# Moved fills, a tile and a buffer more, and gates one tile early in a hybrid recurrent layer on one core

## The chip, the cores and the metric

The kernel runs on one core of one Trainium2 chip. The metric is the device time of one execution in microseconds; the time given is the median of several runs. Engines are called by the names of the profile: PE (TensorE, matmul), DVE (VectorE), ACT (ScalarE), POOL (GpSimd) and SP (SyncE, which issues nearly all the DMAs).

## What is computed

One layer of a decoder, float32, for two groups of tokens: a prompt of 256 tokens and 8 samples of 8 tokens each, 320 token columns in all. Cut to what matters here:

```python
h = rms_norm(x, norm_g)                       # x: 320 x 2048
p = h @ w_in                                  # 2048 x 12416: all of both branches' inputs and gates
# branch A (RWKV-7, 16 heads of 64): token shift, low-rank decay and input gate, then per token
#   S = S diag(w) - (S kk)(kk * a)^T + v k^T ;  y = S r
# branch B (HGRN2, 8 heads of 128), per token
#   S = diag(g) S + k v^T ;  o = S^T q
y_a = (group_norm(y) * ln_w + ln_b + bonus) * silu(p[za])
y_b = rms_norm(o, hg_g) * silu(p[zb])
merged = sigmoid(p[GA]) * (y_a @ proj_a) + sigmoid(p[GB]) * (y_b @ proj_b)
y = rms_norm(x + merged @ w_out, final_norm_g)
```

The states of both branches after the last token are outputs too. The samples start from given states (`state_rwkv`, `state_hgrn`), the prompt from zero.

## The kernel before

Activations are kept transposed: 128 channels on the partitions, 320 tokens in the columns. Each float32 product of the large projections is made of three fast products: the weights `raw` are split by ACT into a rounded high part (`whi`) and by DVE into the rest (`wlo`), the activations likewise (`hhi`, `hlo`), and PE adds `whi*hhi`, `whi*hlo` and `wlo*hhi`. One tile of a projection is 128 output columns; its 16 blocks of 128 inputs are 48 matmuls of 128 x 320. Weights come in pieces of 8 blocks (512 KB) into three buffers. The work has four stages.

*Start.* The three pieces of `x` (piece 2 holds the 64 sample tokens) are squared and summed by ACT (`squares`, `scale`), scaled by DVE (`gain`, line 643), transposed by PE (`turn`, line 655), and split into `hhi` (ACT, `high`) and `hlo` (DVE, `low`). Meanwhile POOL builds masks (`mf`, `mk`, `own8`) and then the low parts of the first weights (`half`, line 750; `divide`, line 535). The order on PE, ACT, DVE and POOL is written out by hand here. `first` is the first tile of the projection; `fetch(0, 0, 1)` loads the next weights into a buffer as soon as POOL has finished with it. A run of fills (lines 700 to 709) writes constants into tiles that the recorded stage uses later: `yz`, `xc`, `qz`, halves of `lora_lw` and `lora_la`, and the masks `rs_a` and `rs_b` of the scans.

*Recorded stage* (lines shown as L199 in the profile, whichever function issues them). 71 tiles of the input projection stream through PE, and between them goes the work of eight pairs: two heads of branch A (`rwkv(p, ...)`) and one of branch B (`hgrn(p, ...)`) each. All instructions are first recorded with their reads and writes, and `Recorder.order` then plans one order for each engine and the SP queue from the dependences, a cost for each instruction and the rank of what hangs on it. For a POOL operation of this kind its cost line is

```python
o.cost = 950 if "dma" in name else 95 + free * 0.88 if name == "memset" else (330 if name == "tensor_copy" and free > 9 else 200) + free * 1.66
```

to which 20 is added and 65 taken off. Tiles of branch A come from `at(...)`: a tag with `bufs` buffers that go round; calls with the same tag share them. Small products go to PSUM banks whose tiles are all called `bank` in the profile.

In `rwkv`, `s0` is the state of the eight samples: loaded by SP, transposed by PE (`ps0`), scaled in place by DVE, added to, and stored by SP. The scaling factors reach the right places through PE: POOL writes them on diagonals (`fd`, 128 x 256, twice for each pair, from `fq`), and PE multiplies `jr_sum` with `fd` into `pf`. At the end of a pair the output `py` is split into `yh` and `yl` (high and low part), which PE multiplies with `jr_cent`; squares are split into the same two tiles, and PE multiplies them with `jr_mean`. `yl` takes the tag `fd`, which has one buffer.

*Projections and gates* (lines 1616 to 1641). The outputs `ya` and `yb` are split (`split`: `yah`, `yal`, `ybh`, `ybl`). Then follow 16 tiles of 128 output channels. For each: gate A (`ga`; the first seven were computed in the recorded stage, stored to `late`, and are loaded here), gate B (`gbt`, a tile of the input projection and a sigmoid of three ACT steps), the projection of A (`ppa`), that of B (`ppb`), and the merge on DVE and ACT (`mt`, `mhi`, `mlo`, `ms`).

*Output projection* (lines 1662 to 1781), with the residual and the last norm.

Of the kernel before, what the change touches and what calls it, by code (L numbers as in the profile page):

```python
# [9 lines left out]
F32 = mybir.dt.float32  # L10
F32R = mybir.dt.float32r
# [6 lines left out]
NP_ = 256  # L18
NS = 64
NT = NP_ + NS  # L20
NSEQ = 8
LS = 8
KT = D // 128
# [404 lines left out]
def hybrid_step(ctx, tc, x_prompt, x_sample, state_rwkv, state_hgrn, state_shift, norm_g, w_in,  # L428
# [4 lines left out]
    V, S, G, T = nc.vector, nc.scalar, nc.gpsimd, nc.tensor  # L433

    S.add_instruction(mybir.InstLoadActFuncSet(
        name=nc.get_next_instruction_name(), act_func_set_id=EXP_LN_SET, ins=[], outs=[]))
# [11 lines left out]
    def ctile(shape, name, dt=F32, pool=rconst):  # L448
        return pool.tile(shape, dt, name=name, tag=name)
# [12 lines left out]
    lora_lw = ctile([128, NT], "lora_lw", F32R)  # L462
    lora_la = ctile([128, NT], "lora_la", F32R)
# [3 lines left out]
    HS = [slice(0, 64), slice(64, 128)]  # L467
# [18 lines left out]
    def project(dst, w, c0, nk, xhi, xlo, pre=()):  # L486

        for k8 in range(nk // 8):
            hi, lo = pre[k8] if k8 < len(pre) else weights(load(w, c0, k8))
            for q in range(8):  # L490
                k = 8 * k8 + q
                T.matmul(dst, hi[:, q, :], xhi[:, k, :], start=(k == 0), stop=False)  # L492
                T.matmul(dst, hi[:, q, :], xlo[:, k, :], start=False, stop=False)  # L493
                T.matmul(dst, lo[:, q, :], xhi[:, k, :], start=False, stop=(k == nk - 1))  # L494
                yield

    def run(gen):
        for _ in gen:
            pass
# [3 lines left out]
    def main(c0, post, pre=()):  # L503
        ps = psm.tile([128, 512], F32, name="mps", tag="m")
        yield from project(ps[:, :NT], win, c0, KT, hhi, hlo, pre)
        post(ps[:, :NT])


    with tc.tile_pool(name="start", bufs=1) as st, \
# [21 lines left out]
        def divide(b_, n, sub):  # L531
            for j in range(n):
                ks = slice(8 * j // n, 8 * (j + 1) // n)
                S.copy(whi[b_][:, ks], wraw[b_][:, ks])
                sub.tensor_sub(wlo[b_][:, ks], wraw[b_][:, ks], whi[b_][:, ks].bitcast(F32))
            return whi[b_], wlo[b_]
# [132 lines left out]
        def warm(n):  # L669
            for _ in range(n):  # L670
                T.matmul(wps[:, :256], ones[:, :128], ones, start=True, stop=True)

        tps = {}
        with tc.manual_schedule(engines={mybir.EngineType.PE, mybir.EngineType.Activation, mybir.EngineType.DVE,
# [20 lines left out]
            yz = ctile([128, 2, 2, 2, 64], "yz")  # L695
            xc = ctile([128, 4, 32], "xc")
            qz = ctile([128, NSEQ, 32], "qz")
            arp = ctile([128, 5, 2, 2, 64], "arp")
            for t_ in (yz, xc, qz, lora_lw[HS[1]].bitcast(F32), lora_la[HS[0]].bitcast(F32)):
                V.memset(t_, 0.0)  # L700


            rs_a = ctile([128, NT], "rs_a")
            rs_b = ctile([128, NT], "rs_b")
            V.memset(rs_a, 1.0)
            V.memset(rs_a[:, 0:NP_:64], 0.0)
            V.memset(rs_a[:, NP_::8], 0.0)
            V.memset(rs_b, 1.0)
            V.memset(rs_b[:, ::8], 0.0)
            warm(20)  # L710
            squares(2)
            scale(2)
# [26 lines left out]
            def first(part, k4):  # L739

                w, x = ((whi, hhi), (whi, hlo), (wlo, hhi))[part]
                for k_ in range(4 * k4, 4 * k4 + 4):
                    T.matmul(first_ps[:, :NT], w[k4 // 2][:, k_ % 8], x[:, k_], start=part == 0 and k_ == 0,
                             stop=part == 2 and k_ == KT - 1)
# [39 lines left out]
            first(1, 2)  # L784
            first(2, 2)
            divide(2, 1, G)
            V.memset(arp, 0.0)
            ps = pst.tile([128, 512], F32, name="cps", tag="t")
            T.transpose(ps[:, :128], rows, ident)
# [29 lines left out]
    def sigm(out, in_, bias=0.0, sign=1.0):  # L819

        S.activation(out, in_, AF.Exp, scale=-sign, bias=bias)
        S.activation(out, out, AF.Ln, bias=1.0)
        S.activation(out, out, AF.Exp, scale=-1.0)
# [12 lines left out]
    def ring(pool, tag, shape, bufs, dt, size, clear=False):  # L836

        if (pool.name, tag) not in rings:
            n_ = size or math.prod(shape[1:])
            if tag in SHARED:  # L840
                rings[pool.name, tag] = [0, [wide_[:, SHARED[tag]:SHARED[tag] + n_]]]
                if clear:
                    G.memset(wide_[:, 384:], 0.0)
        if (pool.name, tag) not in rings:
            rings[pool.name, tag] = [0, [pool.tile([128, n_], dt, name=f"{tag}_{j}", tag=f"{tag}_{j}")
                                         for j in range(bufs)]]
            for t_ in rings[pool.name, tag][1]:
                if clear:
                    G.memset(t_ if dt == F32 else t_.bitcast(F32), 0.0)
        r_ = rings[pool.name, tag]  # L850
        t_ = r_[1][r_[0] % len(r_[1])]
        r_[0] += 1
        t_ = t_[:shape[0], :math.prod(shape[1:])]
        if len(shape) == 2:
            return t_
        names = "abcdef"[:len(shape) - 1]
        return t_.rearrange(f"p ({' '.join(names)}) -> p {' '.join(names)}", **dict(zip(names, shape[1:])))
# [7 lines left out]
    def at(name, shape=(128, NT), tag=None, bufs=1, dt=F32):  # L865
        tag = tag or name
        return ring(pa, tag, list(shape), bufs, dt, SIZES.get(tag), tag in CLEAR)
# [48 lines left out]
    def rwkv(p, r, k, v, za):  # L916
# [6 lines left out]
        for dst, own, other in ((wst, HS[0], HS[1]), (ast, HS[1], HS[0])):  # L923
            S.copy(dst[own], w2a2[own])
            V.tensor_sub(dst[other], w2a2[own], dst[own].bitcast(F32))
        s0 = at("s0", (128, NSEQ, 64))
        Y.dma_start(s0, state_rwkv[0, :, 2 * p:2 * p + 2].rearrange("s h v k -> (h v) s k"))

        kk = at("kk", (128, 3, 128), tag="uK").rearrange("p a b -> p (a b)")[:, :NT]
# [141 lines left out]
        for i in range(1, 7):  # L1071
            m = 7 - i
            t_ = at("t3", (128, 5, i, m), tag="big")
# [6 lines left out]
        t_ = at("t3", (128, 4, 8, 8), tag="big")  # L1080
        V.tensor_mul(t_, within(0, [264, 4], [32, 8], [1, 8]), own8[:, None, None, :].to_broadcast([128, 4, 8, 8]))
        V.tensor_reduce(column(0, [40, 4], [1, 8]), t_, axis=mybir.AxisListType.X, op=ALU.add)
        for d_ in range(1, 4):
            n, m = 4 - d_, 8 * d_
            pw_ = at("pw_", (128, n, 8), tag="uK")
            t_ = at("t3", (128, n, 8, m), tag="big")
            V.tensor_mul(t_, within(8, [264, n], [32, 8], [1, m]), column(32 * d_ + 8, [40, n], [0, 8], [1, m]))
            V.tensor_reduce(pw_, t_, axis=mybir.AxisListType.X, op=ALU.add)
            t_ = at("t3", (128, n, 8, 8), tag="big")
# [41 lines left out]
        V.tensor_mul(bon, pbn[:, :NT], v)  # L1131

        yh = at("yh", dt=F32R)
        yl = at("yl", tag="fd", dt=F32R)

# [124 lines left out]
        for sp in range(4):  # L1262
            for h, o_, w in parts4:
                t_ = NP_ + 16 * sp
# [320 lines left out]
    with tc.manual_schedule():  # L1585
# [4 lines left out]
        V, S, G, T, Y = (book.proxy(e) for e in ("V", "S", "G", "PE", "Y"))  # L1590
        record_all()
        V, S, G, T = real
# [15 lines left out]
    fpr = prj.enter_context(tc.tile_pool(name="fpr", bufs=1))  # L1608
    psf = prj.enter_context(tc.tile_pool(name="psf", bufs=2, space=PSUM))

    def split(y, name, pool, tag):
        hi = pool.tile([128, 8, NT], F32R, name=name + "h", tag=tag)
        lo = fpr.tile([128, 8, NT], F32R, name=name + "l")
        for g in range(4):
            gs = slice(2 * g, 2 * g + 2)
            S.copy(hi[:, gs], y[:, gs])
            V.tensor_sub(lo[:, gs], y[:, gs], hi[:, gs].bitcast(F32))  # L1617
        return hi, lo

    yah, yal = split(ya, "ya", fpr, "yah")  # L1620
    ybh, ybl = split(yb, "yb", ypool, "ya")
    for m in range(KT):
        ga = fpr.tile([128, NT], F32, name="ga", tag="ga", bufs=2)
        if m < NLATE:
            nc.sync.dma_start(ga, late[m])
        else:
            run(main(OFF_GA + 128 * m, lambda ps: sigm(ga, ps)))
        gbt = fpr.tile([128, NT], F32, name="gbt", tag="gbt", bufs=2)
        run(main(OFF_GB + 128 * m, lambda ps: sigm(gbt, ps)))
        ps = psf.tile([128, 512], F32, name="ppa", tag="f")  # L1630
        run(project(ps[:, :NT], proj_a[0], 128 * m, 8, yah, yal))
        mt = fpr.tile([128, NT], F32, name="mt", tag="mt", bufs=2)
        V.tensor_mul(mt, ga, ps[:, :NT])
        ps = psf.tile([128, 512], F32, name="ppb", tag="f")
        run(project(ps[:, :NT], proj_b[0], 128 * m, 8, ybh, ybl))
        V.tensor_mul(gbt, gbt, ps[:, :NT])
        V.tensor_add(mt, mt, gbt)
        S.copy(mhi[:, m, :], mt[:, :NP_])
        V.tensor_sub(mlo[:, m, :], mt[:, :NP_], mhi[:, m, :].bitcast(F32))
        S.copy(ms[:, m, 0], mt[:, NP_:])  # L1640
        V.tensor_sub(ms[:, m, 1], mt[:, NP_:], ms[:, m, 0].bitcast(F32))
# [64 lines left out]
    with tc.manual_schedule(engines={mybir.EngineType.PE}):  # L1706
        for n in range(3):
            pts = out_tiles(n)
            for kk in range(8):
# [16 lines left out]
                if step % 2 == 1 and 9 <= step < 23:  # L1726
                    t_ = len(tail)
# [82 lines left out]
```

## Time and profile before

| | |
|---|---|
| median of 3 runs | 1065.17 us (1065.13 to 1065.8) |
| the profiled execution | 1065.99 us, its span 1063.8 us |
| PE busy | 1045.8 us, 98% of the span, 8740 matmuls |
| DVE, ACT, POOL busy | 763.5, 697.9, 127.8 us |
| granted PE clock | 0.997 |

Line numbers are those of the kernel before. In a row of the timeline the columns are start, duration, engine, line, operation, output <- inputs, shape and count; the bracket at the end gives the idle time of that engine just before and what ended it. In a list of waits they are who waited, for whom, and then microseconds in all, times and the longest.

### The profile page before, as it was taken

What the parts mean: (1) busy time and instruction counts of PE and PEld (TensorE: products, weight loads), DVE (VectorE), ACT (ScalarE), POOL (GpSimd) and SP (SyncE); (2) the same over time, 40 slices, a digit from 0 to 9 for tenths busy, and PEclk for the clock granted to TensorE, in tenths of its full rate; (3) what the DMA queues carried; (4) which work ended last, traced back from release to release, by engine and by line L of the source; (5) the groups of instructions that cost most, each with busy time, mean ns of one, the idle gap of its engine ahead of it and who ended that gap; (6) DMA issues with size and microseconds to landing.
All of it is one profiled execution on the core that took longest, in us unless ns stands there. A gap on an engine that the chain in (4) does not pass through costs nothing.

```text
span 1063.8 us, 23012 instructions
## 1 busy us (share of the span) xinstructions
PE 1045.8 (98%) x8740; PEld 1010.4 (95%) x8740; DVE 763.5 (72%) x1616; ACT 697.9 (66%) x1608; POOL 127.8 (12%) x361
## 2 busy tenths in 40 slices
PE   7999999999999999999999999999999999999996
PEld 6999999999999999999999999999999999988885
DVE  8789989999999898998988857444444444446532
ACT  7757878978879689788687787444444444445412
POOL 9511201212112013112011000000000000000000
PEclk9999999999999999999999999999999999999998
DMA  6776585684865856849757647555555555497402
GB/s 202 198 184 163 126 228 142 162 224 121 216 165 123 223 147 171 210 115 214 184 139 194 175 115 219 170 165 148 156 145 152 152 146 155 144 296 266 152 17 99
DMA packets 356370, 178.78 MB, mean 168 GB/s; under 512 B 82013, under 2 KB 345440, under 8 KB 355684
## 3 DMA queue, kind: packets, MB, share of 16 engines
q1 hardware_dynamic: 355892, 176.01, 60.4%
q8 instruction: 68, 1.11, 0.4%
q10 hardware_dynamic: 368, 1.31, 0.3%
q14 instruction: 42, 0.34, 0.1%
HBM read 159.97 MB, written 17.32 MB: 167 GB/s over the span
## 4 chain that ended last, share of the span: by engine, by line
PE 94%; POOL 2%; ACT 1%; DVE 1%; DMA 1%; issue 0%; DVEq 0%; ACTq 0%; POOLq 0%
PE mps L199 47%; PE bank L199 10%; PE mps L494 5%; PE mps L493 5%; PE mps L492 5%; PE po L1682 3%; PE po L1681 3%; PE po L1683 3%; PE ppb L493 2%; PE ppb L494 2%; PE ppb L492 2%; PE ppa L494 2%; PE ppa L493 2%; PE ppa L492 2%; PE po L1687 1%; PE po L1686 1%
## 5 line engine op out<-in xcount | busy, mean ns | idle before, releaser
L199 PE MATMUL mps<-hhi,whi 128*128 128x320 f32 x1136 | 356.7, 314 | 0.0
L199 PE MATMUL mps<-hlo,whi 128*128 128x320 f32 x1136 | 355.7, 313 | 0.0
L199 PE MATMUL mps<-hhi,wlo 128*128 128x320 f32 x1136 | 354.7, 312 | 0.0
L199 PEld LDWEIGHTS mps<-hhi,whi 128*128 128x128 f32 x1136 | 213.6, 188 | 3.2 <-issue 2.3
L199 PEld LDWEIGHTS mps<-hlo,whi 128*128 128x128 f32 x1136 | 213.7, 188 | 1.2 <-issue 0.4
L199 PEld LDWEIGHTS mps<-hhi,wlo 128*128 128x128 f32 x1136 | 213.6, 188 | 1.1 <-issue 0.4
L199 DVE TENSOR_TENSOR wlo<-raw,whi 128x1024 fp32r<-128x1024 f32 x140 | 171.4, 1224 | 23.2 <-ACT whi L199 21.7
L482 ACT CAST whi<-raw 128x1024 fp32r<-128x1024 f32 x82 | 86.0, 1048 | 148.5 <-PE mps L493 93.7
L483 DVE TENSOR_TENSOR wlo<-raw,whi 128x1024 fp32r<-128x1024 f32 x82 | 100.4, 1225 | 113.3 <-ACT whi L482 113.1
L199 ACT CAST whi<-raw 128x1024 fp32r<-128x1024 f32 x140 | 146.2, 1044 | 44.0 <-PE mps L199 34.1
L493 PE MATMUL mps<-hlo,whi 128*128 128x320 f32 x400 | 123.6, 309 | 0.0
L494 PE MATMUL mps<-hhi,wlo 128*128 128x320 f32 x400 | 123.6, 309 | 0.0
L492 PE MATMUL mps<-hhi,whi 128*128 128x320 f32 x400 | 123.6, 309 | 0.0
L492 PEld LDWEIGHTS mps<-hhi,whi 128*128 128x128 f32 x400 | 75.1, 188 | 0.0
L493 PEld LDWEIGHTS mps<-hlo,whi 128*128 128x128 f32 x400 | 75.1, 188 | 0.0
L494 PEld LDWEIGHTS mps<-hhi,wlo 128*128 128x128 f32 x400 | 75.1, 188 | 0.0
L1670 DVE TENSOR_TENSOR wlo<-raw,whi 128x1024 fp32r<-128x1024 f32 x32 | 38.6, 1222 | 36.7 <-ACT whi L1669 36.5
L1669 ACT CAST whi<-raw 128x1024 fp32r<-128x1024 f32 x32 | 33.1, 1051 | 47.6 <-PE po L1686 21.7
L1681 PE MATMUL po<-whi,mhi 128*128 128x512 f32 x128 | 50.0, 391 | 0.0
L1683 PE MATMUL po<-wlo,mhi 128*128 128x512 f32 x128 | 50.0, 391 | 0.0
L1682 PE MATMUL po<-whi,mlo 128*128 128x512 f32 x128 | 50.0, 391 | 0.0
L493 PE MATMUL ppb<-ybl,whi 128*128 128x320 f32 x128 | 39.7, 310 | 0.4 <-DVE ybl L1617 0.4
(415 smaller groups left out, 1986.3 us busy)
## 6 DMA issues: line engine op xcount, KB each, us to landing
raw<-in_w_in_dram SPq DMA_DIRECT2D x194, 512.0 KB
raw<-in_w_out_dram SPq DMA_DIRECT2D x32, 512.0 KB
raw<-in_proj_a_dram SPq DMA_DIRECT2D x16, 512.0 KB
raw<-in_proj_b_dram SPq DMA_DIRECT2D x16, 512.0 KB
s<-in_state_hgrn_dram SPq DMA_DIRECT2D x8, 512.0 KB
ww<-scr SPq DMA_DIRECT2D x8, 512.0 KB
out_dram<-s SPq DMA_DIRECT2D x8, 512.0 KB
scrt<-ww SPq DMA_DIRECT2D x32, 120.0 KB
```

Of the source, the lines that this page charges most:

```text
L199: o.fn(*(real(x) for x in o.args), **{k: real(x) for k, x in o.kw.items()})
L482: S.copy(hi[:, ks], raw[:, ks])
L483: sub.tensor_sub(lo[:, ks], raw[:, ks], hi[:, ks].bitcast(F32))
L492: T.matmul(dst, hi[:, q, :], xhi[:, k, :], start=(k == 0), stop=False)
L493: T.matmul(dst, hi[:, q, :], xlo[:, k, :], start=False, stop=False)
L494: T.matmul(dst, lo[:, q, :], xhi[:, k, :], start=False, stop=(k == nk - 1))
L1669: S.copy(hi, raw)
L1670: V.tensor_sub(lo, raw, hi.bitcast(F32))
L1681: T.matmul(pt, h, hi, start=first, stop=False)
L1682: T.matmul(pt, l, hi, start=False, stop=False)
L1683: T.matmul(pt, h, lo, start=False, stop=end)
L1686: T.matmul(pt, h, hi, start=first, stop=False)
```

## The change

Four edits. The ten fills of lines 700 to 709 are issued after the last `hlo` step and the division of the third weight piece, ahead of the fill of `arp`, in place of before the scaling of `x`; all of them stay on DVE. `yl` gets a tile of its own. `s0` of branch A gets two buffers. In the projection stage the gates of tile m + 1 are issued ahead of the projections of tile m, and `ga` and `gbt` get three buffers.

```diff
@@ start
             arp = ctile([128, 5, 2, 2, 64], "arp")
-            for t_ in (yz, xc, qz, lora_lw[HS[1]].bitcast(F32), lora_la[HS[0]].bitcast(F32)):
-                V.memset(t_, 0.0)
             rs_a = ctile([128, NT], "rs_a")
             rs_b = ctile([128, NT], "rs_b")
-            V.memset(rs_a, 1.0)
-            V.memset(rs_a[:, 0:NP_:64], 0.0)
-            V.memset(rs_a[:, NP_::8], 0.0)
-            V.memset(rs_b, 1.0)
-            V.memset(rs_b[:, ::8], 0.0)
             warm(20)
             squares(2)
...
             divide(2, 1, G)
+            for t_ in (yz, xc, qz, lora_lw[HS[1]].bitcast(F32), lora_la[HS[0]].bitcast(F32)):
+                V.memset(t_, 0.0)
+            V.memset(rs_a, 1.0)
+            V.memset(rs_a[:, 0:NP_:64], 0.0)
+            V.memset(rs_a[:, NP_::8], 0.0)
+            V.memset(rs_b, 1.0)
+            V.memset(rs_b[:, ::8], 0.0)
             V.memset(arp, 0.0)
@@ rwkv
-        s0 = at("s0", (128, NSEQ, 64))
+        s0 = at("s0", (128, NSEQ, 64), bufs=2)
...
-        yl = at("yl", tag="fd", dt=F32R)
+        yl = at("yl", dt=F32R)
@@ projections and gates
-    for m in range(KT):
-        ga = fpr.tile([128, NT], F32, name="ga", tag="ga", bufs=2)
+    def gates(m):
+        ga = fpr.tile([128, NT], F32, name="ga", tag="ga", bufs=3)
         if m < NLATE:
             nc.sync.dma_start(ga, late[m])
         else:
             run(main(OFF_GA + 128 * m, lambda ps: sigm(ga, ps)))
-        gbt = fpr.tile([128, NT], F32, name="gbt", tag="gbt", bufs=2)
+        gbt = fpr.tile([128, NT], F32, name="gbt", tag="gbt", bufs=3)
         run(main(OFF_GB + 128 * m, lambda ps: sigm(gbt, ps)))
+        return ga, gbt
+
+    made = [gates(0)]
+    for m in range(KT):
+        if m + 1 < KT:
+            made.append(gates(m + 1))
+        ga, gbt = made[m]
         ps = psf.tile([128, 512], F32, name="ppa", tag="f")
```

## The prediction

> **What bounds the kernel now.** I read the page first: the span, the share of TensorE (PE), the chain that ended last.
>
> ```profile
> span 1063.8 us, 23012 instructions
> PE 1045.8 (98%) x8740; PEld 1010.4 (95%) x8740; DVE 763.5 (72%) x1616; ACT 697.9 (66%) x1608; POOL 127.8 (12%) x361
> PE 94%; POOL 2%; ACT 1%; DVE 1%; DMA 1%; issue 0%; DVEq 0%; ACTq 0%; POOLq 0%
> ```
>
> PE carries the time. No edit removes a matmul, so the change can win only where PE stands still. Second view: the table by stage.
>
> ```profile
> 87.80:648.00 560.20, 558.37 (x5678) 546.13 (x5678) 497.67 (x1214) 460.50 (x1224) 84.94 (x252) 1.00 0.66 171
> 648.00:666.00 18.00, 17.30 (x116) 16.77 (x115) 13.54 (x17) 13.03 (x21) 0.00 (x0) 1.00 0.73 203
> 666.00:948.00 282.00, 282.00 (x1900) 280.26 (x1899) 124.89 (x156) 121.83 (x181) 0.00 (x0) 1.00 0.56 162
> ```
>
> The columns are the window, its length, then PE, weight loads, DVE, ACT and POOL busy. The recorded stage loses 1.8 us of PE, the turn to the projections 0.7, the tile loop nothing. Its 282.00 us over 1900 matmuls are 0.148 us a step, while a matmul is shown 0.31 long (rows below): ends overlap, so a stall costs its idle time plus about 0.16. Third view: who PE waited for.
>
> ```profile
> PE bank L199 <- POOL fd L199: 1.5, 3, 0.6
> PE bank L199 <- DVE wst L199: 0.4, 1, 0.4
> ...
> PE ppb L493 <- DVE ybl L1617: 0.4, 1, 0.4
> PE bank L199 <- issue: 0.4, 1, 0.4
> PE ppa L493 <- DVE yal L1617: 0.3, 1, 0.3
> ```
>
> Three of the four edits touch rows of this list; that list is nearly all there is to win.
>
> **Edit 1: the fills move behind the scaling of x.**
>
> ```profile
> 7.01 0.48 DVE L700 MEMSET yz<- 128x512 f32 x1
> ...
> 9.71 1.30 DVE L643 SCALAR_TENSOR_TENSOR xt<-xt,ssq,gb 64x1024 f32<-64x1024 f32 x1
> 9.71 0.09 DVE L709 MEMSET rs_b<- 128x40 f32 x1
> ...
> 8.92 0.20 ACT L638 ACTIVATE ssq<-ssq 64x1 f32<-64x1 f32 x1
> ...
> 13.85 0.20 ACT L638 ACTIVATE ssq<-ssq 128x1 f32<-128x1 f32 x1
> ...
> 17.17 0.67 DVE L663 TENSOR_TENSOR hlo<-tps,hhi 128x512 fp32r<-128x512 f32 x1
> ...
> 9.43 0.19 POOL L596 TENSOR_TENSOR own<-own,ident 128x8 f32<-128x8 f32 x1
> 9.59 1.51 POOL L570 TENSOR_SCALAR_AFFINE_SELECT mf<-mf 32x16 f32<-32x16 f32 x3
> 11.07 7.62 POOL L596 TENSOR_TENSOR own<-own,ident 128x8 f32<-128x8 f32 x6
> 18.65 2.54 POOL L750 TENSOR_TENSOR wlo<-raw,whi 128x512 fp32r<-128x512 f32 x2
> ...
> 11.07 6.23 POOL L596 TENSOR_TENSOR own<-own,ident 128x8 f32<-128x8 f32 x1
> ...
> 20.34 0.75 PE L743 MATMUL mps<-hhi,wlo 128*128 128x320 f32 x4
> ...
> 21.22 4.25 DMA raw<-in_w_in_dram
> ...
> 29.10 0.20 DVE L199 RECIPROCAL lbt<-lbt 128x8 f32<-128x8 f32 x1 [2.93 <-ACT lbt L199]
> ```
>
> Ten fills hold DVE from 7.01 to 9.80, 2.8 us, the time of the whole move; no other queue is passed, and no DMA moves. The first scaling needs `ssq`, ready at 8.92 + 0.20 = 9.12, so it can start at about 9.16 instead of 9.71: 0.55 earlier. The later scalings follow back to back, but those of the third piece of x need the `ssq` that ACT finishes at 14.05, and their place moves from 14.5 to 14.0: some 0.1 is lost, and `hlo` starts at 16.7 instead of 17.17. Left alone, PE would be 0.45 earlier.
>
> It is not left alone. While DVE scales, POOL stands: one add of 8 columns takes 6.23 us, from 11.07 to 17.30, when the last of eight scalings is over (`hlo` starts at 17.17), though the scaling shown lasts 1.30. Today POOL clears one add (9.43) and two of the three `mf` steps before it is caught, and the third `mf` step after the first scaling; with the scalings at 9.16 it is caught at the add of 9.43. From the two rows of adds, five of them take 7.62 - 6.23 = 1.4 us, 0.28 each. After the release, now at about 16.85, come the three `mf` steps (about 0.15 each when free) and six adds instead of five: `wlo` starts at 16.85 + 0.45 + 1.65 = 18.95, against 18.65. PE reads it at 20.34 today and would be there at 19.9; the first `wlo` half (2.54 / 2) is ready at 20.2. So PE gains 0.1 there, and the queue behind is worse off: the second half frees `raw`, which SP reloads (4.25 us, 21.22), and ACT, the shifted columns and `wst` hang on it. PE's wait for `wst` ends 0.2 to 0.3 later, and that is the place where the start ends for PE. I take +0.2. The ends are -0.45 (POOL is no later than DVE) and +1.5 (POOL misses its slot after the release by one more operation of 1.3).
>
> The Trainium skill, page "SBUF — State Buffer", section "Who interferes with whom", says that a DVE instruction with two SBUF inputs and a GpSimd one that reads SBUF exclude each other for a whole instruction, and the second to issue waits until the first finishes. The 6.23 us row agrees that they exclude each other and differs on the end: the add sat out seven scalings, not one. By that rule an add would slip in at each boundary, and edit 1 would give -0.45.
>
> The fills' new place: behind them on DVE stand `arp`, the copies of `cols` and `sst` and the first steps of `bounds`, up to the reciprocal at 29.10. DVE idles 2.93 us before that one, for ACT's `lbt`, and the fills' 2.8 us use that hole up, while no other engine asks DVE for anything. So 0; without the hole the chain to `wst`, and PE, would be 2.8 us later.
>
> **Edit 2: `yl` gets its own tile.** `fd` (POOL) feeds the `pf` products; today it must wait until PE has read the previous pair's `yl`, which sits in the same buffer.
>
> ```profile
> L199 PE MATMUL bank<-fd,jr_mean x1: 306/306/306, 348.4 to 348.4; 128*128 128x320 f32 x1
> ...
> 348.85 1.66 POOL L199 TENSOR_TENSOR fd<-id,fq 128x256 fp32r<-128x256 f32 x1 [6.84 <-PE bank L199]
> ...
> 350.56 0.38 PE L199 MATMUL bank<-fd,jr_sum 128*128 128x256 f32 x1 [0.43 <-POOL fd L199]
> ...
> 425.73 1.43 POOL L199 TENSOR_TENSOR fd<-id,fq 128x256 fp32r<-128x256 f32 x1 [1.04 <-PE bank L199]
> ...
> 427.21 0.39 PE L199 MATMUL bank<-fd,jr_sum 128*128 128x256 f32 x1 [0.40 <-POOL fd L199]
> ...
> 576.83 0.39 PE L199 MATMUL bank<-fd,jr_sum 128*128 128x256 f32 x1 [0.64 <-POOL fd L199]
> ...
> L199 POOL TENSOR_TENSOR fd<-id,fq x16: 614/618/1662, 50.4 to 577.3; 128x256 fp32r<-128x256 f32 x16
> ```
>
> At 348.4 PE reads `yl`, at 348.85 POOL may fill `fd`, and PE stands at 350.56. The stalls at 350.56 and 576.83 are of this kind, first `fd` of a pair: (0.43 + 0.16) + (0.64 + 0.16) = 1.4 us. The one at 427.21 is at the pair's second `fd`, which POOL began only when the first one's product had let its buffer go (1.04 idle, one buffer still): 0.40 + 0.16 stays. All three stalls come where POOL took 1.4 to 1.7 us instead of 0.62; the planner's cost line gives an `fd` 0.58 (200 + 256 x 1.66 ns, + 20 - 65). So -1.4. Ends: -2.0 (all three go) and 0 (as many return elsewhere). What is late next: the second `fd`.
>
> **Edits 2 and 3 also re-plan.** The order of the recorded stage is computed from the dependences, so two released buffers can move every instruction in it. Seven pairs today:
>
> ```profile
> 372.30:444.30 72.00, 71.60 (x724) 69.96 (x723) 64.80 (x160) 60.84 (x162) 13.10 (x36) 1.00 0.69 178
> 444.30:515.01 70.71, 70.71 (x720) 69.23 (x719) 62.68 (x158) 55.12 (x147) 12.45 (x36) 1.00 0.66 168
> sum 499.23, PE 497.40 PEld 486.09 DVE 454.87 ACT 410.43 POOL 84.37; mean PE 71.06 PEld 69.44 DVE 64.98 ACT 58.63 POOL 12.05
> ```
>
> Mean 71.32, extremes 70.71 and 72.00. All seven at the best would be -4.3, all at the worst +4.8 (stalls of edit 2 included); seven independent draws of about 0.5 spread by 1.3. I take 0, nearest to the mean, and keep 1.3 for the range.
>
> **Edit 3: two buffers for `s0`.** The next pair's state load no longer waits for the store of this one.
>
> ```profile
> SPq L199 <- DMA out_dram<-s: 4.2, 3, 2.4
> ```
>
> SP stood 4.2 us for state stores, weight loads queued behind it, but PE's list has no wait for a weight load. Seven loads of 256 KB can be issued earlier, past weight loads. So 0; the ends are -0.6 (the stall at "issue", which nothing here explains, 0.4 + 0.16) and +0.6 (one such load puts a weight tile late once, priced by the same row). The transposes of `s0` are on nobody's list of PE waits.
>
> **Edit 4: the gates a tile early.** In the loop PE is full, so there the order is worth 0. At its entrance it is not:
>
> ```profile
> 654.98 0.31 PE L492 MATMUL ppa<-yah,whi 128*128 128x320 f32 x1
> 655.63 0.41 PE L493 MATMUL ppa<-yal,whi 128*128 128x320 f32 x1 [0.34 <-DVE yal L1617]
> ...
> 651.81 1.05 ACT L482 CAST whi<-raw 128x1024 fp32r<-128x1024 f32 x1 [1.42 <-DMA raw<-in_proj_b_dram]
> 659.05 3.02 DVE L1617 TENSOR_TENSOR ybl<-yb,ybh 128x640 fp32r<-128x640 f32 x4
> ```
>
> After gate tile 0 PE needs `yal` and `ybl`, which come late. With gate tile 1 ahead, 48 steps of 0.148 or 7.1 us later, `ppa` starts at 662.1 and `ppb` at 665.6; `ybl` is complete at 662.07. Both stalls (0.34 here, 0.4 in the list) go: 0.34 + 0.4 + 2 x 0.16 = -1.0. What must be there sooner is gate tile 1's weights: they take the places in ACT and DVE that the two projections' weights hold today, the second cast at 651.81 against a need at 658.5. SP issues the seven `ga` loads one tile earlier, past the weight loads of two projections; each needs the buffer of a tile that is done, as today, so what queues behind them on SP (weights) waits no longer. ACT's three sigmoid steps and the gate's PSUM bank move with the tile. Ends -1.0 and 0 (the splits slide behind the weights).
>
> **Sum.** +0.2 - 1.4 + 0 + 0 - 1.0 = -2.2 us. The profiled execution took 1065.99 (span 1063.8 and 2.2 around it), so 1063.8; the median of the runs, 1065.17, lies 0.8 below that execution, so 1062.9, 0.21% less. The bound of "no change", 0.2% or 2.1 us (about what a measurement of this kernel can tell from none), is 1063.0: my forecast stands on that edge.
>
> **The rivals.**
> *Everything listed goes*: all three `fd` stalls (2.0), both split stalls (1.0), and the wait for `wst` (0.4 + 0.16): 1065.17 - 3.6 = 1061.6. For it: earlier `fd` means slack. Against it: edit 1's POOL chain.
> *POOL slips in between scalings*: edit 1 gives -0.45, 1062.3. For it: one `mf` step did end between the first two scalings (9.59 + 1.51 = 11.10). Against it: the 6.23 us. The Trainium skill's page "SBUF — State Buffer", section "Who interferes with whom", would lead here.
> *The `fd` stalls move, not vanish*: a planner that prices at 0.58 what took up to 1.66 places the product as tightly somewhere else; edit 2 is worth 0 and the time is 1065.17 + 0.2 - 1.0 = 1064.4. For it: the price is unchanged. Against it: the first `fd` now has nothing to wait for but `fq`.
> *Slower*: `fd` moves early into the stretch where DVE works without pause on two SBUF operands, and POOL is kept out as at 11.07. If in pairs 1 to 7 the product waits 1.66 - 0.62 = 1.04 each, 7.3 us replace today's 2.0: 1065.17 + 0.2 - 1.0 - 2.0 + 7.3 = 1069.7. It decides from 4.9 us of such waits in all (2.1 + 2.0 + 1.0 - 0.2), 0.7 a pair. Against it: 13 of 16 `fd` today cost PE nothing.
>
> **How the numbers follow.** Forecast 0.42, split 0.26 below and 0.16 above 1063.0 by the re-plan's spread; everything goes 0.15; POOL slips in 0.07; stalls move 0.25; slower 0.11. Faster 0.26 + 0.15 + 0.07 = 0.48, same 0.16 + 0.25 = 0.41, slower 0.11. The range runs from 1061.2 (the best case, less 0.4 of the re-plan's spread) to 1065.7 (stalls move, plus the re-plan's 1.3); it leaves out the slower case and some 0.06 at the ends.
>
> **What would show it.** Edit 1: the first scaling at 9.2, the long POOL add ending near 16.85, `wlo` L750 starting near 18.95, PE's `wst` wait ending near 37.6. Edit 2: first `fd` of a pair released by `fq`, no PE stall at it. Edit 3: no SP wait for the store of `s`. Edit 4: gate tile 1 before the first `ppa`, both split stalls gone from PE's list. I am wrong if PE's list grows a new wait over 1 us, or if the pairs' mean leaves 70.7 to 71.6.

## The result and the profile after

The changed kernel takes 1071.89 us (median of 4 runs, 1071.36 to 1072.73) against 1065.24 for the kernel before on the same chip: a ratio of 1.006, interval 1.0048 to 1.0072. It is 6.6 us slower; 2.2 us faster was forecast, and the value lies above the whole range. Lines of the profile page after:

```profile
span 1071.0 us, 22985 instructions
PE 1049.7 (98%) x8740; PEld 1010.9 (94%) x8740; DVE 758.6 (71%) x1616; ACT 696.7 (65%) x1608; POOL 128.8 (12%) x361
```

The matmuls are the same 8740. Where the time lies shows in the table by stage, cut where the stream of the recorded stage begins and ends: first before, then after (window, length, then PE, weight loads, DVE, ACT and POOL busy).

```profile
26.80:647.90 621.10, 618.84 (x6100) 606.00 (x6099) 546.39 (x1320) 501.01 (x1307) 103.77 (x305) 1.00 0.67 172
647.90:1063.80 415.90, 406.42 (x2514) 386.41 (x2512) 193.92 (x245) 177.13 (x268) 0.00 (x0) 0.99 0.53 159
```

```profile
26.10:656.00 629.90, 622.67 (x6100) 606.19 (x6099) 543.06 (x1325) 499.32 (x1305) 105.38 (x305) 1.00 0.66 170
656.00:1071.00 415.00, 406.20 (x2514) 386.32 (x2512) 194.15 (x245) 177.02 (x268) 0.00 (x0) 0.99 0.53 160
```

The start gained 0.7 (its stream begins at 26.1, not 26.8), everything behind the recorded stage gained 0.9, and the recorded stage lost 8.8: +7.2 together, which is the difference of the spans. The stage does the same 6100 matmuls at the same clock; PE's idle time in it (length less busy) went from 2.3 to 7.2 us. That is 5.0 of the 8.8 us; the other 3.8 are busy time of the same matmuls, since one that starts late is shown whole and no longer overlaps with the one before (the 0.16 us a stall of the prediction). Set against the median step from one operation to the next of the same kind, taken over all fourteen traces, 55 steps before and 75 after come over 0.1 us late, by 10.2 and 17.8 us together. The list of PE's waits after:

```profile
PE bank L199 <- DVE es L199: 3.8, 3, 1.9
PE bank L199 <- DVE rl L199: 2.2, 2, 1.8
PE mps L199 <- DVE wlo L199: 0.7, 2, 0.5
```

The wait for `fd` is gone, and so are those for `yal` and `ybl`. In their place stand waits for DVE (`es`, `rl`, `wlo`), on code that no edit touches. The best and the worst of the seven whole pairs, and their sum, which was 499.23:

```profile
86.85:160.24 73.39, 71.49 (x721) 69.39 (x719) 64.02 (x162) 59.59 (x157) 11.19 (x36) 1.00 0.66 168
...
450.04:521.58 71.54, 71.27 (x720) 69.36 (x719) 60.07 (x152) 56.48 (x150) 11.27 (x36) 1.00 0.63 159
...
sum 508.00, PE 500.99 PEld 486.56 DVE 452.81 ACT 409.63 POOL 86.44; mean PE 71.57 PEld 69.51 DVE 64.69 ACT 58.52 POOL 12.35
```

The mean pair went from 71.32 to 72.57, outside the 70.7 to 71.6 that the prediction had set as its own test. Before, the worst pair took 72.00; now four of the seven take more.

One chain can be followed in the timeline of after (SP, ACT, DVE and PE, a fence each). SP loads `bk`, the copies into `big` stand 4.06 us for it, the scan behind them stands 4.43, DVE then works without a pause up to `es`, and PE stands for that:

```profile
72.30 0.59 SPq L199 DMA_DIRECT2D bk<-scrt  x1
```

```profile
79.39 0.40 ACT L199 ACTIVATE big<-bk,seq 128x128 f32<-128x128 f32 x1 [4.06 <-DMA bk<-scrt]
```

```profile
80.19 0.82 DVE L199 TENSOR_TENSOR_SCAN F<-rs_b,w 128x320 f32<-128x320 f32 x1 [4.43 <-ACT w L199]
```

```profile
97.39 0.33 PE L199 MATMUL bank<-ident,es 128*128 128x128 f32 x1 [1.88 <-DVE es L199]
```

It looks like a cause: a load that lands later than its place in the order allows. ACT's waits for `bk` grew from 0.7 us to 13.3. Whether it is the cause was left to the experiments.

### The profile page after: what moved, and what is told of

Same layout as the page of the kernel before. It is cut to its first block, busy times and chain, and to the rows that moved or that the text cites. A ratio compares the mean times of both kernels' runs of the same rounds, so it can differ in the third digit from the quotient of the medians.

```text
span 1071.0 us, 22985 instructions
## 1 busy us (share of the span) xinstructions
PE 1049.7 (98%) x8740; PEld 1010.9 (94%) x8740; DVE 758.6 (71%) x1616; ACT 696.7 (65%) x1608; POOL 128.8 (12%) x361
## 3 DMA queue, kind: packets, MB, share of 16 engines
q10 hardware_dynamic: 368, 1.31, 0.3%
## 4 chain that ended last, share of the span: by engine, by line
PE 46%; DMA 2%; DVE 1%; ACT 1%; issue 0%; DVEq 0%; SPq 0%; ACTq 0%
PE mps L199 9%; PE mps L493 5%; PE mps L492 5%; PE mps L494 5%; PE bank L199 2%; DMA raw<-in_w_out_dram 2%; PE po L1688 2%; PE po L1686 2%; PE po L1687 2%; PE ppb L493 2%; PE ppa L493 2%; PE ppb L492 2%; PE ppa L492 2%; PE ppb L494 2%; PE ppa L494 2%; PE po L1691 1%
## 5 line engine op out<-in xcount | busy, mean ns | idle before, releaser
L492 PE MATMUL ppa<-yah,whi 128*128 128x320 f32 x128 | 39.6, 309 | 0.0
```

## The experiments

Five theories. *P*: the order that the planner wrote for the recorded stage is what costs; the edits as such do what was forecast. *R* (the rival): the released buffers cost by themselves, because loads and POOL work start earlier and collide. *B*: the planner's price for the `bk` load is too low, and that alone spoils the new order. *D*: the prices of all loads are too low. *L*: nothing in the new order is special; the order of before lies at the good end of what the planner gives, and any new plan is a draw. (The first expectation below uses R for another rival, that the moved fills disturb the recorded stage.) All runs were timed against the kernel before on the same chip; that kernel's medians there were 1066.85, 1066.57 and 1066.62 us, so only ratios are compared across chips. Line numbers move by up to three with the edits.

**One part alone.** Three kernels: edits 1 and 4 (the fills and the gates; neither touches the dependences of the recorded stage), edit 2, edit 3. Each is the kernel before with these lines of the change:

```diff
# e1_fills_gates: the hunks "start" and "projections and gates"
# e2_yl_alone
-        yl = at("yl", tag="fd", dt=F32R)
+        yl = at("yl", dt=F32R)
# e3_s0_alone
-        s0 = at("s0", (128, NSEQ, 64))
+        s0 = at("s0", (128, NSEQ, 64), bufs=2)
```

> Edits 1 and 4 alone (fills moved, gates a tile early); yl and s0 share buffers as before, so the recorded stage keeps the order of before. Theory P (the new order of the recorded stage costs the time): the start gives 0.7 to 1.0 us and the entrance to the projections 0.9 to 1.0, so 1063.4 us, and the window of the recorded stage is as long as before, 621 us. Rival R (the moved fills disturb the recorded stage, whose first operations they delay on VectorE): the recorded stage is longer by several us and the time is 1068 to 1072.

> Edit 2 alone: yl in a tile of its own. Theory P: the planner may now place the fd products of a pair without the end of the pair before, so the order of the whole recorded stage changes; if yl is the edit that does it, 1068 to 1074 us with ScalarE waiting for the bk load several times. Rival: yl alone is harmless and takes the fd stalls away, 1063 to 1064 us, and s0 is the culprit.

> Edit 3 alone: two buffers for s0 of branch A. Theory P: a new order here too, with a cost of a few us either way; if s0 is the culprit 1069 to 1073 us and TensorE waits for es and rl. Rival: s0 alone moves one load and nothing else, 1065.2 us plus or minus 1.

Measured: 0.9984 (0.9975 to 0.9993), 0.9988 (0.9978 to 0.9998) and 1.0008 (0.9999 to 1.0018). In microseconds of 1066.85 that is -1.7, -1.3 and +0.9. The three sum to -2.1, which is nearly the forecast, and nowhere near +6.4: no part carries the loss by itself. The recorded stage took 621.7 us with edits 1 and 4, so the moved fills don't disturb it. Edits 2 and 3 each bring a new order; there it took 619.9 and 622.7 us.

**All four edits in the order of before.** The planner is told under which buffer names the dependences of before would arise, while the kernel keeps the new tile and the second buffer. The order of the recorded stage is then that of `e1_fills_gates`.

```diff
+        self.alias = {}
...
+                if t_.name in self.alias:
+                    self.spans[key] = self.alias[t_.name], *self.spans[key][1:]
...
+            if pool.name == "pa" and tag in ("fd", "yl", "s0"):
+                for t_ in rings[pool.name, tag][1]:
+                    book.alias[...] = "s0" if tag == "s0" else "fd"
```

> All four edits with their tiles and buffers, but the planner is told that yl still lies in fd and that s0 has one buffer, so it writes out the order of before. Theory P: the time is that of edits 1 and 4 alone or a little less, 1062 to 1064 us; the fd stalls, which come with that order, stay. Rival R (the freed buffers themselves cost, by earlier loads or other places in memory): 1069 us or more.

Measured: 0.9978 (0.9969 to 0.9988), -2.4 us; forecast of the direct effects: -2.2. Its table by stage and the sum of its seven pairs:

```profile
27.20:648.30 621.10, 619.35 (x6100) 606.20 (x6099) 546.74 (x1325) 499.62 (x1301) 101.35 (x305) 1.00 0.68 172
648.30:1063.10 414.80, 405.86 (x2514) 386.36 (x2512) 194.06 (x245) 177.17 (x268) 0.00 (x0) 1.00 0.53 160
```

```profile
sum 499.45, PE 497.83 PEld 486.21 DVE 453.33 ACT 410.87 POOL 82.59; mean PE 71.12 PEld 69.46 DVE 64.76 ACT 58.70 POOL 11.80
```

Same instructions, tiles and buffers as the changed kernel, 621.1 us for the recorded stage instead of 629.9. The 8.8 us are the order's alone (the ratios, 0.9978 and 1.006, say 8.7): P stands, and R falls. Against the expectation, most of the `fd` stalls went too (see edit 2 below).

**What the new order has wrong: the `bk` load.** After with one price changed, so that `bk` is planned 3 us earlier ahead of its use:

```diff
+                if tuple(out.shape) == (128, 5, 128):
+                    o.lat = 7500
```

> The changed kernel, with one price of the planner altered: it counts 7.5 us from the issue of the bk load to its landing in place of 4.5 (the trace of the changed kernel shows 5.8 to 7.4). Theory B (the new order puts ScalarE's bm copies right at a landing that comes later than planned; ScalarE stands, VectorE and then TensorE stand after it): ScalarE's waits for the bk load, 13.3 us in all there, fall to 3 or less, TensorE's stalls in the recorded stage from 6.7 to under 3, and the time is 1064 to 1066.5 us. Theory L (any new order is a draw, the bk waits are a symptom): the time can land anywhere from 1063 to 1072, without going with the bk waits.

Measured: 1.0032 (1.002 to 1.0043), recorded stage 628.3. ACT's list of waits, first after, then this kernel, and behind them this kernel's longest wait of PE in the recorded stage:

```profile
ACT big L199 <- DVE uK L199: 15.9, 5, 3.9
ACT big L199 <- DMA bk<-scrt: 13.3, 5, 4.1
ACT whi L199 <- DMA raw<-in_w_in_dram: 11.8, 7, 4.0
```

```profile
ACT whi L201 <- DMA raw<-in_w_in_dram: 28.9, 18, 3.8
...
ACT big L201 <- DMA bk<-scrt: 1.7, 1, 1.7
```

```profile
PE bank L201 <- DVE es L201: 4.0, 3, 1.6
```

The wait for `bk` fell from 13.3 to 1.7, and PE waits for `es` as long as before (3.8, now 4.0); ACT's waits for weights grew in its stead, from 11.8 to 28.9. So the loss doesn't need the waits for `bk`: B falls. Only 1.6 of the 8.8 us of the stage came back (3.0 us by the ratios, 1.006 and 1.0032). Since this price gives the rest of the stage another order too, the run doesn't show what the chain above cost within the order of after.

**Draws.** Two constants of the planner are nudged: the slack by which an instruction that isn't ready yet may be preferred (`AHEAD`, 300 to 320 ns) and what is added to each DVE, ACT and POOL cost (`SPARE`, 20 to 22 ns). Neither means anything at this size except another order. Two of the kernels carry all four edits, two only edits 1 and 4, with the dependences of before:

```diff
# e6_shake_after_ahead (all edits), e12_shake_edits14_b (edits 1 and 4)
-    AHEAD, SLIP, SOON, SPARE = 300, 0, 1500, 20
+    AHEAD, SLIP, SOON, SPARE = 320, 0, 1500, 20
# e7_shake_after_spare (all edits), e8_shake_edits14 (edits 1 and 4)
-    AHEAD, SLIP, SOON, SPARE = 300, 0, 1500, 20
+    AHEAD, SLIP, SOON, SPARE = 300, 0, 1500, 22
```

> The changed kernel with an indifferent constant of the planner moved (AHEAD, the ns by which an engine may wait for a better operation, 300 to 320), which gives another order from the same dependences. Theory B: the bk price is as wrong as before, so ScalarE still waits for bk 8 us or more in all and the time stays at 1069 to 1073. Theory L: a fresh draw, 1063 to 1072; far from 1071.9 it speaks for L.

> The same with another indifferent constant (SPARE, the ns added to each operation of VectorE, ScalarE and POOL, 20 to 22). Theory B: again 1069 to 1073 with 8 us or more of bk waits. Theory L: a second fresh draw, 1063 to 1072.

> Edits 1 and 4 alone (buffers shared as before), SPARE 20 to 22: a new order from the old dependences. Theory B: the old dependences keep the bm copies late, few bk waits (under 3 us), 1063 to 1067 us. Theory L: a draw like the others, and a loss of 3 to 7 us against edits 1 and 4 with their own order is as likely as with the freed buffers.

> Edits 1 and 4 alone, AHEAD 300 to 320: a second new order from the old dependences. Theory L: 1065 to 1076, as likely bad as the shaken orders of the freed buffers. Theory B (the freed buffers themselves invite bad orders): close to edits 1 and 4 in their own order, within 2 us.

Measured: 1.0103 (1.0087 to 1.0118), 1.004 (1.0025 to 1.0055), 1.0043 (1.0029 to 1.0056), 1.0057 (1.0042 to 1.0072); recorded stage 634.2, 625.9, 628.6 and 630.8. The two kernels with the dependences of before are as bad as the changed one, though nothing but the order differs from `e1_fills_gates` (621.7). What PE waits for is another thing each time: `wlo` (6.2 us) in the first, an idle time that the profile ends with "issue" (2.4) in the second, and in the two others the samples' state, which has one buffer in these two; no order of 620 to 622 us contains that wait. Nor do the waits of ACT for `bk` go with the length of the stage, as B had it: they are 18.5, 3.9, 0.6 and 14.2 us in these four. Rows of `e8_shake_edits14` and `e12_shake_edits14_b`:

```profile
PE bank L199 <- DMA s<-in_state_rwkv_dram: 4.0, 4, 1.7
PE bank L199 <- issue: 1.1, 2, 0.6
```

```profile
PE bank L199 <- DMA s<-in_state_rwkv_dram: 4.4, 3, 2.1
```

**All loads planned 2 us earlier** (D), with `SPARE` at 20 and at 22:

```diff
-            o.cost, o.lat = 380, 5500
+            o.cost, o.lat = 380, 7500
...
-                o.lat = 6500 if out.shape[-1] == 1024 else 4500
+                o.lat = 8500 if out.shape[-1] == 1024 else 6500
```

> The changed kernel, with the planner's landing time of every load and store raised by 2 us (5.5, 4.5 and 6.5 become 7.5, 6.5 and 8.5). Theory D (new orders are bad because their slack against late landings is planned too short, whatever the landing; bk was only one of them): waits of ScalarE and VectorE for DMAs, 29 us in the changed kernel, fall to under 12, the recorded stage from 630 us to 618 to 622 and the time to 1061 to 1065. Theory L (every re-plan is a draw, and the order of before a good one): 1065 to 1076, as the four re-plans so far.

> The same with SPARE at 22, so another order. Theory D: good again, within 2 us of the run beside it. Theory L: it differs from it by several us, as orders from neighbouring constants did before.

Measured: 1.0061 (1.0046 to 1.0076) and 1.0122 (1.0107 to 1.0137). The weight stream of the recorded stage ends 626.8 and 629.3 us after its begin, but in these two kernels some 110 matmuls of the stage come only behind that end, between those of the gates. The window behind it holds 2624 matmuls, not 2514 (first kernel):

```profile
653.40:1072.00 418.60, 409.94 (x2624) 389.72 (x2622) 199.91 (x260) 183.53 (x289) 0.00 (x0) 0.99 0.53 159
```

Counted like the others (the span, less what lies ahead of the stream and less the 414.7 us that the other kernels with edit 4 need behind it), the stage takes about 631 and 636 us. A little of that is the clock: these two executions were granted 0.994 and 0.993, before 0.997; one run of the first kernel at 0.997 took 1071.26 us, still 4.6 above before. The waits of ACT for `bk` and weights in the first fell from 25.1 us in after to 4.5, and PE's list moved on to ACT:

```profile
PE mps L199 <- ACT whi L199: 2.4, 1, 2.4
PE mps L199 <- ACT za L199: 1.8, 1, 1.8
PE mps L199 <- ACT pad L199: 1.4, 2, 0.7
```

The DMA waits fell as D had said and the stage got no shorter, so D falls too.

**Edits 1, 2 and 4**, the changed kernel without the second buffer for `s0`:

```diff
-        s0 = at("s0", (128, NSEQ, 64), bufs=2)
+        s0 = at("s0", (128, NSEQ, 64))
```

> Edits 1, 2 and 4 without the second buffer of s0, so in the order that yl alone gave. If time is the sum of the stages: the recorded stage of yl alone (619.9 us against 621.1 of before) with the start and the entrance of edits 1 and 4 (0.2 to 0.7 and 1.0): 2.4 to 3 us under the kernel before, ratio 0.997 to 0.998, the best so far. Theory L agrees, as the order is the one already drawn. If the order of a stage interacts with when its start is ready, it is at 0.999 or above.

Measured: 0.9977 (0.9967 to 0.9986), -2.5 us, recorded stage 620.7, rest 414.5: the stages add up as expected. With the version in the order of before (0.9978) it is the fastest here, and both beat the kernel before as well as the changed one.

**The draws together.** The middle column says how much of the order of before is left: the share of ACT's and of DVE's instructions in the recorded stage that keep their sequence, worked out from the two traces by the longest matching stretches of tile names. It is a rough measure, as the names are the same in every pair. The stage lengths are of one execution each; the order of before gives 621.1 to 621.7.

| kernel | order of before kept, ACT / DVE | recorded stage, us |
|---|---|---|
| edits 1 and 4; all edits in the old order | 1.00 / 1.00; 1.00 / 0.99 | 621.7; 621.1 |
| edit 2; edits 1, 2 and 4 | 0.63 / 0.57; 0.63 / 0.57 | 619.9; 620.7 |
| edit 3 | 0.47 / 0.39 | 622.7 |
| after; `bk` earlier | 0.35 / 0.41; 0.32 / 0.43 | 629.9; 628.3 |
| after, 320; after, 22 | 0.34 / 0.29; 0.27 / 0.42 | 634.2; 625.9 |
| edits 1 and 4, 22; the same, 320 | 0.31 / 0.35; 0.29 / 0.36 | 628.6; 630.8 |
| loads earlier; the same, 22 | 0.16 / 0.24; 0.24 / 0.28 | about 631; about 636 |

The eight orders that keep about a third or less of ACT's sequence need 625.9 to about 636, 630.5 in the mean; those that keep about half or more need 619.9 to 622.7 (DVE's share doesn't part them: 0.39 with edit 3, 0.41 after). That fits L: the order of before is a good one, small departures kept its quality, and a plan that starts over loses 5 to 15 us, with the dependences of before as with the new ones. The small departures are only two orders, that of edit 2, timed twice, and that of edit 3. The table shows that the two go together, not why. What makes an order good is open: the stage is worse each time by another wait, and no price tried cured it. Nor does a run show why the order in use is a good one, whether by luck or because the planner's constants were chosen with it.

## Why the prediction was wrong, step by step

**The step that failed** is the paragraph "Edits 2 and 3 also re-plan", with its "I take 0, nearest to the mean, keep 1.3 for the range". The term measured +8.8 us (621.1 against 629.9 with all else equal). The mechanism was named and its size mis-set, and the bound with it: "all seven at the worst" gave +4.8. Seven pairs inside one order are seven samples of that order; I took their spread for the spread between orders. Nor was 0 its middle: the ten new orders tried here average about 628.7 us, 7.6 above before. The profile gave a hint: a stage that idles 2.3 us in 621 leaves little room for a better order, and much for a worse one. The slower rival (1069.7) came nearest in size, by another way: PE's list after has no wait for `fd`.

**Edit 1** (+0.2, ends -0.45 and +1.5). The first scaling starts at 8.86 (9.2 was forecast; 8.86 to 9.98 in the eleven traces with this edit). `hlo` starts at 16.46, and the fills use up DVE's idle time ahead of the reciprocal, as forecast: 0.28 of it is left of 2.93. POOL came out otherwise. DVE's and POOL's timelines after, then POOL's in `e2_yl_alone`, whose start is that of before:

```profile
8.86 7.68 DVE L643 SCALAR_TENSOR_TENSOR xt<-xt,ssq,gb 64x1024 f32<-64x1024 f32 x8 [1.89 <-ACT ssq L638]
16.46 4.87 DVE L663 TENSOR_TENSOR hlo<-tps,hhi 128x512 fp32r<-128x512 f32 x8
...
28.12 0.20 DVE L199 RECIPROCAL lbt<-lbt 128x8 f32<-128x8 f32 x1 [0.28 <-ACT lbt L199]
```

```profile
9.09 2.34 POOL L570 TENSOR_SCALAR_AFFINE_SELECT mf<-mf 32x16 f32<-32x16 f32 x2
11.41 1.25 POOL L596 TENSOR_TENSOR own<-own,ident 128x8 f32<-128x8 f32 x1
12.62 2.02 POOL L570 TENSOR_SCALAR_AFFINE_SELECT mf<-mf 32x16 f32<-32x16 f32 x3
14.62 2.82 POOL L596 TENSOR_TENSOR own<-own,ident 128x8 f32<-128x8 f32 x6
17.40 3.78 POOL L741 TENSOR_TENSOR wlo<-raw,whi 128x512 fp32r<-128x512 f32 x3
```

```profile
11.20 5.71 POOL L596 TENSOR_TENSOR own<-own,ident 128x8 f32<-128x8 f32 x6
16.87 4.28 POOL L750 TENSOR_TENSOR wlo<-raw,whi 128x512 fp32r<-128x512 f32 x3
```

After, nine mask operations of POOL begin before the last scaling ends at 16.54, and `wlo` starts at 17.40 instead of the 18.95 forecast. That is not the edit's doing: in `e2_yl_alone` and `e3_s0_alone`, which start like before, POOL slips in between the scalings as well, and `wlo` starts at 16.87 and 16.77. The add of 6.23 us, on which this part of the forecast rested, stands in one trace of fourteen. Nor did it cost PE anything that shows: before, with `wlo` at 18.65, reads `wst` at 37.37 and begins its recorded stage at 26.8; the other two, with `wlo` 1.8 earlier, read `wst` at 37.43 and 36.96 and begin the stage at 27.5 and 27.0. So the step from a late `wlo` to a late PE isn't borne out either. With the edit the stage begins at 26.1 to 27.2 in eleven traces, against 26.8 to 27.5 in the three without; single traces overlap, and about -0.5 is what they show. That is the size that the rival "POOL slips in between scalings" had.

**Edit 2** (-1.4). Right about the stalls, not shown in the time; best seen with the order held. PE's waits for `fd` with edits 1 and 4 alone, and its timeline at the two `fd` products of pair 5 with all four edits in that same order:

```profile
PE bank L199 <- POOL fd L199: 1.5, 3, 0.7
```

```profile
426.53 0.28 PE L202 MATMUL bank<-fd,jr_sum 128*128 128x256 f32 x1
...
428.37 0.39 PE L202 MATMUL bank<-fd,jr_sum 128*128 128x256 f32 x1 [0.39 <-POOL fd L202]
```

Of three stalls one is left, at the pair's second `fd`, 0.39 us where 0.40 was forecast to stay. The time fell by less: in this order the stage went from 621.7 to 621.1 and the ratio from 0.9984 to 0.9978, about 0.6 us for edits 2 and 3 together, no more than two traces of one order differ by. Other waits stand in PE's list with all four edits in the old order:

```profile
PE bank L202 <- issue: 0.6, 2, 0.4
PE bank L202 <- DVE es L202: 0.4, 1, 0.4
...
PE bank L202 <- POOL fd L202: 0.4, 1, 0.4
PE bank L202 <- DVE rl L202: 0.3, 1, 0.3
```

In the new order no wait for `fd` is in PE's list at all. "First `fd` of a pair released by `fq`" holds in part; where POOL's idle time ahead of `fd` ended, after:

```profile
  DVE fq L199: 20.6, 5
  PE bank L199: 9.1, 6
```

**Edit 3** (0, ends -0.6 and +0.6). With its own new order it measured +0.9, interval -0.1 to +1.9. What was forecast for SP, no wait for the store of `s`, did not come. Its list after, and the loads of the state (column four onwards: ns, then first and last start):

```profile
SPq L199 <- DMA out_dram<-s: 6.6, 4, 3.4
```

```profile
L199 SPq DMA_DIRECT2D s<-in_state_rwkv_dram x8: 389/590/1348, 27.4 to 501.4; - x8
```

The last load of branch A's state is issued at 501.4; it was issued at 567.6 before. SP's wait for stores stayed (4.2 before): all four waits of after end at a load of branch B's state, `s` in the profile too, which still has one buffer, and so do the three of before. I had put the row down to branch A.

**Edit 4** (-1.0). Right in its mechanism, and worth a little more. The first `ppa` comes 14.1 us, two gate tiles, behind the end of the recorded stage, and no wait for `yal` or `ybl` is left (PE after):

```profile
670.12 0.31 PE L492 MATMUL ppa<-yah,whi 128*128 128x320 f32 x1
670.27 0.31 PE L493 MATMUL ppa<-yal,whi 128*128 128x320 f32 x1
```

The time behind the recorded stage is 414.2 to 415.0 in eight kernels with this edit (415.8 in a ninth, and the two of D left out), 415.9 to 416.7 in the three without: about -1.5.

So the terms other than the re-plan summed to -2.2 in the forecast and to -2.4 (-3.3 to -1.2) on the chip. That they agree is in part luck: about -0.5 for +0.2, -0.6 for -1.4 and -1.5 for -1.0 cancel. One term set at 0 decided.

## What to carry to other kernels

Where an order is computed from dependences, a released buffer is two changes, the buffer and a new order of everything; price the second by other orders of the same work, not by the spread inside the one you have, and where the present order idles hardly at all, reckon with a loss (eight of ten new orders here). Hold the order while you try an edit (tell the planner the old dependences): here that split +6.4 us into -2.4 and +8.8 in one run. And a chain that ends at a stall is a suspect, not a cause: take its first wait away and see whether the stall goes, and remember that a new plan changes more than that wait.

## What the runs showed of the hardware

How long POOL is held by a streak of DVE steps can differ between executions of the same start. In thirteen of the fourteen traces POOL got an operation or more through between scalings, and none of its mask operations was held longer than 1.31 us, about one scaling (1.30 in the row of before); in `e2_yl_alone` the six adds took 5.71 us (row above). In before, with the same start as there, one add was held 6.23 us, through seven scalings. The rule that the Trainium skill gives on the page "SBUF — State Buffer", sections "Who interferes with whom" and "Summary: rules for kernel authors" (the second to issue waits until the first finishes), fits the thirteen and doesn't fit the 6.23 us of before. One execution of fourteen says that the longer hold can happen, not how often.
